# Layer 0's group roots as split pairs, parameters in the rows of the first input tile, the last norm's weight applied ahead of its root, and 500 tries in the planner

## The chip, the core and the metric

The kernel runs on one core of one Trainium2 chip. The metric is the device time of one execution in microseconds (us); lower is better. Each time given is the median of several executions. Beside it stands one profiled execution, whose rows are read below.

The engines have short names in the profile: PE is TensorE (matrix products into PSUM), PEld its weight loads, DVE is VectorE, ACT is ScalarE, POOL is GpSimd, SP is SyncE, which here issues nearly all DMAs.

## What is computed

A decoder trunk of two layers on 1024 tokens of 1024 channels in float32. Each layer: an RMS norm, one input projection whose columns feed four token mixers (a: latent attention, b: gated convolution, c: multi-scale pooling, d: sliding-window attention), an RMS norm of each mixer's 256 channels, one output projection, a residual; then an RMS norm, a gated feed-forward block, a residual. A last RMS norm ends it.

```python
for l in range(DEPTH):
    h = rmsnorm(x, attn_norm[l])
    proj = h @ w_in[l]
    ...
    groups = jnp.stack([y_a, y_b, y_c, y_d], axis=2)
    gf = groups.astype(jnp.float32)
    gf = gf * lax.rsqrt(jnp.mean(gf * gf, axis=-1, keepdims=True) + RMS_EPS)
    mixed = (gf.reshape(b, s, D_MIX) * mix_norm[l].astype(jnp.float32)).astype(x.dtype)
    x = x + mixed @ w_o[l]
    h2 = rmsnorm(x, ffn_norm[l])
    gate, up = jnp.split(h2 @ w_gate_up[l], 2, axis=-1)
    x = x + (jax.nn.silu(gate) * up) @ w_down[l]
return rmsnorm(x, final_norm)
```

## The kernel before

**Layout.** Channels lie on the 128 partitions, tokens on the free axis, in two halves of 512 (`HT`). A tile is 128x512 in float32, 256 KB. `x` is eight such tiles (`k`) in each half (`t`). Tiles live in 47 slots of 128x2x512 each (`u0` to `u46`); `F.pair()` takes a slot, `F.half()` half of one, and a half that is freed goes to the next caller.

**Split products.** A float32 value is carried as a pair: `hi`, the value cast to the fp32r type on ACT (L363, or L368 where a gain is multiplied in), and `lo`, the rest, made by a subtraction on DVE (L366, or L369 with the gain). `mm3` (L343) then makes each product of three: hi by hi, hi by lo, lo by hi. So nearly every PE row of the profile is L343.

**Norms.** `SumSq.add` squares tiles on ACT (L398, L407) and sums them on DVE (L415, and L409 for the last, which adds the epsilon). `rnorm` sums over the partitions by a product with a matrix of ones and then takes the reciprocal root: Ln, Exp and Square on ACT (L432 to L434), two steps on DVE (L435, L438). The document calls that product with ones the root's product. It has two forms. With `pair` false it is one product of plain float32 (L426). With `pair` true the sum is split into hi and lo first (ACT, then DVE), and two fp32r products with `ones_r` follow (L423). In layer 1 all group norms are pairs; in layer 0 group b is, while groups c and d (`group_scale`) and the query rank (`sq_q`) use the plain form, for each half of the tokens.

**Start.** A short series of products of ones (L562, 12 of them, two rows each in the trace) runs first on PE. SP loads half of two weight blocks (keys and values, `m` = 2, 3), the first x tile, a 128x86 table of parameters (`par`: gains, taps, sinks, final norm), then more x tiles, the other weight halves, the weights of `m` = 0 (queries) and the second half of x. ACT and DVE split each x tile with its gain from `par`; PE multiplies it by the key and value weights as it comes.

**End.** The last layer's last products run in two pieces of 256 tokens. After each piece: evacuation (L1792), the square (L429), the root's product (L426, L430), the root, and then `finish`: eight DVE steps that multiply a tile by its gain and the root (L490), with a DMA to the output for every two (L498).

**What sets the order.** The program is traced once, and a planner (`Order`) lays out the order of the instructions on each engine by a list schedule over modelled costs. `improve` then tries changed ranks: `tries` times it picks a modelled wait of PE, perturbs the ranks of the 45 us around it, and keeps the change if the modelled span is not longer. This runs twice (`SLOW`), and the better order is imposed on the program. DMA loads are instructions of SP, and their order is planned with the rest. SP has eight DMA lanes: the ninth issue waits until the first has landed.

Of the kernel before, what the change touches and what calls it, by code (L numbers as in the profile page):

```python
# [14 lines left out]
F32 = mybir.dt.float32  # L15
# [5 lines left out]
P = 128  # L21
# [23 lines left out]
WARM = 12  # L45
# [80 lines left out]
def trunk_kernel(ctx: ExitStack, tc: tile.TileContext, ins, out, given=None, ends=None):  # L126
# [17 lines left out]
    par = cpool.tile([P, L * PC_N + NK], F32, name="par")  # L144
# [236 lines left out]
    class SumSq:  # L381
# [35 lines left out]
        def rnorm(self, t, cols=whole, tag="t", final=None):  # L417
# [20 lines left out]
            dve.scalar_tensor_tensor(out=a, in0=q, scalar=1.5, in1=r0, op0=ALU.add, op1=ALU.mult)  # L438
            return self.acc[t]
# [16 lines left out]
    def enter_load(t, k):  # L456
        s = xf[k][t] = F.half()
        sp.dma_start(F.ap(s), x_in[k, :, t * HT : (t + 1) * HT])
# [10 lines left out]
    def first_half(w, i):  # L469

        s = F.half()
        sp.dma_start(F.ap(s), w[2][:, i * HT : (i + 1) * HT])
        w[3].append(s)

    def first_split(w, i):

        cs = slice(i * HT, (i + 1) * HT)
        split(R.ap2(w[0])[:, cs], R.ap2(w[1])[:, cs], F.ap(w[3][i]))
        F.free(w[3][i])

    def first_terms(w, t, k):
        hi, lo = (R.ap2(i)[:, k * P : (k + 1) * P] for i in w[:2])
        return [(hi, lo, R.ap(hh[k][t][0]), R.ap(hh[k][t][1]))]

    def finish(x, t, cols):

        for d in range(NK):
            a = F.ap(x[d][t])[:, cols]
            g = par[:, L * PC_N + d : L * PC_N + d + 1]
            dve.scalar_tensor_tensor(  # L490
                out=a, in0=a, scalar=g, in1=F.ap(ratt[t])[:, cols], op0=ALU.mult, op1=ALU.mult
            )
            ts = slice(t * HT + cols.start, t * HT + cols.stop)
            if t == 0:
                sp.dma_start(out[d, :, ts], a)
            elif d % 2:
                s = slots.cur[x[d][t] // 2]
                sp.dma_start(out[d - 1 : d + 1, :, ts].rearrange("d p n -> p d n"), s[:, :, cols])  # L498

    last_silu = None  # L500
    for l in range(L):
# [57 lines left out]
        if l == 0:  # L559
# [1791 lines left out]
```

## Time and profile before

| what | value |
|---|---|
| median of 3 runs (lowest to highest) | 2038.76 us (2038.35 to 2038.97) |
| the profiled execution, its own time | 2038.94 us |
| its span, from the first to the last instruction | 2037.2 us |
| PE busy / DVE / ACT / POOL | 99% / 76% / 50% / 28% of the span |
| PE instructions | 9422 products, 9422 weight loads |
| moved by DMA | 338.56 MB |
| granted TensorE clock | 0.999 |

How to read the views: the page gives busy times and the chain of work that ended last. The list of waits says which engine waited for which instruction. The timeline merges neighbouring instructions of one line; its columns are the start, the time from the first start to the last end, engine, line and operation, tiles written and read, shape, and the count. Ends of products are modelled, so that neighbouring products overlap in it: the step from one start to the next is what a product costs PE. Windows give the busy time of each engine in a stretch, with the count of instructions, the granted clock, the busy share of the DMA engines and the rate.

### The profile page before, as it was taken

Reading aid. Unit: us, or ns where it says so; the run is one execution under the profiler, and the core shown is the slowest. Engines: PE = TensorE matmul, PEld = TensorE weight load, DVE = VectorE, ACT = ScalarE, POOL = GpSimd, SP = SyncE. Lnnn points to the kernel's source line nnn. Section 1 sums busy time; section 2 is a strip of 40 time slices with the busy share of each in tenths; the row PEclk is TensorE's granted clock in tenths of the full one; section 3 lists DMA queues with packets and bytes.
Section 4 is the critical chain, followed back from the end, with each engine's and each line's share of the span. In section 5 each row is a group of like instructions: output and inputs, shape, how many; then the busy total and the mean of one; then the engine's idle time right before and its main releaser. Section 6 shows DMA issues by size and latency. Waiting matters only on the chain.

```text
span 2037.2 us, 26750 instructions
## 1 busy us (share of the span) xinstructions
PE 2023.3 (99%) x9422; PEld 1677.9 (82%) x9422; DVE 1543.7 (76%) x2449; ACT 1015.1 (50%) x1766; POOL 564.1 (28%) x428
## 2 busy tenths in 40 slices
PE   9999999999999999999999999999999999999998
PEld 7887888878888888888888878888888888888887
DVE  8779979997677778767646898889966766775555
ACT  7447657753333335555533676677433333354342
POOL 0100000047776783000001000000677777710000
PEclk9999999999999999999999999999999999999999
DMA  5531222434555556999835223242454555487552
GB/s 206 106 66 47 72 97 82 155 124 166 187 178 188 177 173 238 367 344 325 283 118 122 63 93 120 92 144 96 146 194 170 194 175 169 160 293 266 182 185 84
DMA packets 154231, 338.56 MB, mean 166 GB/s; under 512 B 15088, under 2 KB 62192, under 8 KB 154096
## 3 DMA queue, kind: packets, MB, share of 16 engines
q1 hardware_dynamic: 149616, 325.31, 46.3%
q0 software_dynamic: 4480, 11.54, 3.2%
q8 instruction: 74, 1.21, 0.2%
q14 instruction: 61, 0.50, 0.1%
HBM read 241.36 MB, written 105.91 MB: 170 GB/s over the span
## 4 chain that ended last, share of the span: by engine, by line
PE 97%; DVE 1%; issue 1%; ACT 0%; DMA 0%; POOL 0%; SPq 0%; DVEq 0%; ACTq 0%; POOLq 0%
PE ps_mm L343 38%; PE ps_s L343 29%; PE ps_t L343 12%; PE ps_pv L343 8%; PE ps_pv L1111 2%; PE ps_t L1099 1%; PE ps_s L1045 1%; PE ps_s L1047 1%; PE ps_s L1046 1%; PE ps_s L659 1%; PE ps_s L917 1%; PE ps_pv L720 1%; PE ps_t L708 1%; PE ps_t L423 0%; DVE u L366 0%
## 5 line engine op out<-in xcount | busy, mean ns | idle before, releaser
L343 PE MATMUL ps_mm<-u,u 128*128 128x512 f32 (+1 forms) x3378 | 831.9, 389 | 2.1 <-ACT u L368 0.7
L343 PEld LDWEIGHTS ps_mm<-u,u 128*128 128x128 f32 x3378 | 616.1, 188 | 125.4 <-issue 2.4
L343 PE MATMUL ps_s<-u,u 128*128 128x512 f32 x2670 | 636.4, 390 | 0.7 <-ACT u L1339 0.5
L366 DVE TENSOR_TENSOR u<-u,u 128x1024 fp32r<-128x1024 f32 (+3 forms) x429 | 493.8, 1174 | 187.4 <-ACT u L363 131.1
L363 ACT CAST u<-u 128x1024 fp32r<-128x1024 f32 (+3 forms) x429 | 370.6, 883 | 443.4 <-PE ps_mm L343 62.8
L343 PEld LDWEIGHTS ps_s<-u,u 128*128 128x128 f32 x2670 | 500.9, 188 | 107.0 <-ACT u L1339 1.3
L343 PE MATMUL ps_t<-u,u 128*128 128x512 f32 (+1 forms) x1124 | 256.3, 378 | 0.1
L343 PEld LDWEIGHTS ps_t<-u,u 128*128 128x128 f32 x1124 | 202.5, 188 | 40.8 <-DVE u L1515 1.5
L1523 POOL TENSOR_TENSOR tp<-tp,u 128x512 f32<-128x512 f32 x80 | 125.0, 1562 | 352.3 <-ACT tp L1521 215.9
L343 PE MATMUL ps_pv<-u,u 128*128 128x512 f32 x744 | 177.1, 389 | 0.0
L343 PEld LDWEIGHTS ps_pv<-u,u 128*128 128x128 f32 x744 | 139.7, 188 | 29.0
L317 POOL DMA_DIRECT2D gd<-in_w_gu x24 | 21.4, 894 | 415.8 <-PE ps_t L343 282.0
L1108 POOL MEMSET u<- 128x128 f32 x32 | 6.3, 223 | 427.4 <-PE ps_pv L1111 117.6
L1521 ACT ACTIVATE tp<-tp 128x512 f32<-128x512 f32 x80 | 50.6, 633 | 129.3 <-DVE tp L442 129.2
L363 ACT CAST u<-ps_t 128x512 fp32r<-128x512 f32 (+3 forms) x132 | 64.7, 503 | 55.4 <-PE ps_t L1099 29.1
L366 DVE TENSOR_TENSOR u<-ps_t,u 128x512 fp32r<-128x512 f32 (+3 forms) x132 | 74.7, 580 | 13.3 <-ACT u L363 12.4
L368 ACT ACTIVATE u<-u,par 128x512 fp32r<-128x512 f32 x100 | 70.2, 717 | 29.2 <-DVE u L442 9.1
L1601 POOL TENSOR_TENSOR u<-u 128x352 f32<-128x352 f32 x64 | 77.0, 1204 | 8.6 <-DMA u<-in_w_dn 8.1
L369 DVE SCALAR_TENSOR_TENSOR u<-u,par,u 128x512 fp32r<-128x512 f32 x100 | 73.2, 746 | 6.3 <-ACT u L368 6.2
L1311 POOL TENSOR_TENSOR u<-u 128x512 f32<-128x512 f32 x38 | 69.9, 1840 | 27.2 <-DVE u L366 25.3
L1601 POOL TENSOR_TENSOR u<-u,u 128x352 f32<-128x352 f32 x64 | 76.4, 1194 | 2.7
L442 DVE TENSOR_TENSOR tp<-tp,u 128x512 f32<-128x512 f32 x76 | 75.3, 990 | 2.0
(204 smaller groups left out, 2314.0 us busy)
## 6 DMA issues: line engine op xcount, KB each, us to landing
u<-in_w_gu SPq DMA_DIRECT2D x84, 512.0 KB, 4.0
ad<-u SPq DMA_DIRECT2D x154, 256.0 KB, 2.4
u<-ad SPq DMA_DIRECT2D x70, 512.0 KB, 5.8
u<-in_w_dn SPq DMA_DIRECT2D x64, 352.0 KB, 3.4
qd<-u SPq DMA_DIRECT2D x64, 352.0 KB, 3.5
u<-in_w_in SPq DMA_DIRECT2D x43, 512.0 KB, 5.3
u<-qd SPq DMA_DIRECT2D x32, 512.0 KB, 5.5
u<-in_w_dn SPq DMA_DIRECT2D x24, 512.0 KB, 5.4
```

Of the source, the lines that this page charges most:

```text
L317: paced(pool.dma_start(d, a, **more))
L343: last_mm = pe.matmul(o, w, r, start=start and k == 0 and i == 0, stop=stop and k == n - 1 and i == 2, skip_group_check=again,)
L363: a = act.copy(hi, f)
L366: dve.tensor_tensor(out=lo, in0=f, in1=rd(hi), op=ALU.subtract)
L368: a = act.activation(hi, f, AF.Copy, scale=gain)
L369: dve.scalar_tensor_tensor(out=lo, in0=f, scalar=gain, in1=rd(hi), op0=ALU.mult, op1=ALU.subtract)
L442: dve.tensor_tensor(out=o, in0=a, in1=b, op=ALU.mult)
L1111: pe.matmul(py[:, c0:], v_of(j, h), R.ap(s)[:, c0:], start=j == 0 and n == 0, stop=j == nj - 1 and n == 1,)
L1311: pool.tensor_tensor(out=q4, in0=q4, in1=F.ap(self.raw[1] + 1), op=ALU.add)
L1521: last_silu = act.activation(g, g, AF.Silu)
L1523: pool.tensor_tensor(out=g, in0=g, in1=r, op=ALU.mult)
L1601: pool.tensor_tensor(out=o, in0=a, in1=b, op=ALU.add)
```

## The change

Four things are changed. (1) Layer 0's groups c and d and the query rank use the pair form of the root's product. (2) `par` is no DMA of its own: its 86 columns stand in DRAM behind the 512 of the first x tile, one DMA loads both (`enter_first`), and DVE copies the columns to `par`. The key and value weights come as four blocks (`w_first[j]`) of two tiles' worth each, and the loads of the first half of x and of these blocks are held in one order by dependencies. Two products of ones fewer run ahead. (3) In the last norm's second half the gain is multiplied in on ACT ahead of the root (`gained`), and `finish_pairs` multiplies two tiles by the root in one DVE step. (4) The planner makes 500 tries, each resumed from a saved state, dropped early if PE is no further along, and kept only if the span is shorter.

```diff
-WARM = 12
+WARM = 10
...
+    def enter_first():
+        s = F.pair()
+        loads.append(sp.dma_start(F.ap2(s)[:, : HT + PC_ALL], ins["first"]))
+        xf[0][0] = s
+        got = F.ap(s + 1)[:, :PC_ALL]
+        hh[0][0] = half_split(F.ap(s), got[:, PC_ATTN : PC_ATTN + 1])
+        dve.tensor_copy(par, got)
+        F.free(s + 1)
...
-            wkv = [(R.pair(), R.pair(), ins["w_in"][0, m], []) for m in (2, 3)]
-            enter_load(0, 0)
-            sp.dma_start(par, ins["params"])
-            for i in range(2):
-                for w in wkv:
-                    first_half(w, i)
-                for k in range(4 * i, 4 * i + 4):
-                    if k:
-                        enter_load(0, k)
+            wkv, wraw, loads = [], [], []
+            for j in range(NK // 2):
+                wraw.append(F.half())
+                loads.append(sp.dma_start(F.ap(wraw[j]), ins["w_first"][j]))
+                if j == 0:
+                    wkv.append(half_split(F.ap(wraw[0])))
+                    F.free(wraw[0])
+                    enter_first()
+                else:
+                    loads.append(enter_load(0, 2 * j))
+                loads.append(enter_load(0, 2 * j + 1))
+            for a, b in zip(loads[1:], loads):
+                behind(a, b)
...
-            sg = SumSq(2 * P, g in ("b", "bcd")[l])
+            sg = SumSq(2 * P, g in "bcd")
...
-        sq_q = SumSq(2 * P, l > 0)
+        sq_q = SumSq(2 * P, True)
...
+    def gained(x, d, cols=whole):
+        a = F.ap(x[d][1])[:, cols]
+        act.activation(a, a, AF.Copy, scale=gain(d))
...
+    def finish_pairs(x, cols):
+        n = cols.stop - cols.start
+        r = F.ap(ratt[1])[:, cols].unsqueeze(1).to_broadcast([P, 2, n])
+        for m in range(NM):
+            s = slots.cur[x[2 * m][1] // 2][:, :, cols]
+            dve.tensor_tensor(out=s, in0=s, in1=r, op=ALU.mult)
+            ts = slice(HT + cols.start, HT + cols.stop)
+            sp.dma_start(out[2 * m : 2 * m + 2, :, ts].rearrange("d p n -> p d n"), s)
...
-            ratt[1] = ss.rnorm(1, cols, tag="s", final=F.ap(x[2 * NM - 2][1])[:, cols])
-            finish(x, 1, cols)
+            a = F.ap(x[2 * NM - 2][1])[:, cols]
+            ratt[1] = ss.rnorm(
+                1, cols, tag="s", final=a, behind=lambda: gained(x, 2 * NM - 2, cols)
+            )
+            finish_pairs(x, cols)
...
-            new = [
-                r + draw.gauss(0.0, 1) if at - 40 < t < at + 5 else r for r, t in zip(rank, end)
-            ]
-            e, o = self.run(new)
-            if max(e) <= span:
+            m = max(0, int((at - 40 * draw.random()) / self.STEP) - 1)
+            far = draw.choice((0.3, 1.0, 3.0))
+            a = marks[m][0]
+            new = [r + draw.gauss(0.0, far) if a < t < at + 5 else r for r, t in zip(rank, end)]
...
+            e, o = self.run(new, since=marks[m], marks=after)
+            if max(e) < span:
...
-            order = plan.improve(best, 30)[1]
+            order = plan.improve(best, 500)[1]
...
+    a["first"] = c(np.concatenate([a["xT"][0, :, :HT], lay.reshape(P, -1), fin], axis=1))
+    two = a["w_in"][0, 2:4].reshape(2, P, NK // 2, 2 * P)
+    a["w_first"] = c(two.transpose(2, 1, 0, 3)).reshape(NK // 2, P, HT)
```

The planner lays out the whole program anew, so nearly every row of every engine stands elsewhere. Three places follow; the names are the program's, with a number for each tile.

**SP, the first loads.** `in_w_in` are weights, `in_xT` tiles of x, `in_params` the table; in brackets stands what the issue waits for, a DMA lane or an engine. Before:

```order
L472 DMA u4_120<-in_w_in 128x512
L458 DMA u4_120<-in_xT 128x512
L565 DMA par_75<-in_params 128x86
L472 DMA u5_124<-in_w_in 128x512
L458 DMA u5_124<-in_xT 128x512
L458 DMA u6_127<-in_xT 128x512 x2
L472 DMA u7_130<-in_w_in 128x512
L458 DMA u8_133<-in_xT 128x512 [waits DMAHW0_49]
```

In the change, where `in_first` is x tile 0 with the table, `in_w_in` the 512 KB of query weights, and the tiles into `u8_138`, `u10_143`, `u11_146`, `u12_149` and `u13_152` are the second half of x:

```order
L580 DMA u0_114<-in_w_first 128x512
L467 DMA u2_119<-in_first 128x598
L591 DMA u9_140<-in_w_in 128x1024
L461 DMA u8_138<-in_xT 128x512
L461 DMA u10_143<-in_xT 128x512 x2
L461 DMA u11_146<-in_xT 128x512 x2
L461 DMA u12_149<-in_xT 128x512 [waits DMAHW0_49]
L461 DMA u12_149<-in_xT 128x512 [waits DMAHW1_49]
L461 DMA u13_152<-in_xT 128x512 [waits DMAHW2_49]
L461 DMA u2_119<-in_xT 128x512 [waits DMAHW3_49,DVE_49]
L580 DMA u4_126<-in_w_first 128x512 [waits DMAHW4_49]
```

The table's own DMA is gone. The second x tile of the first half goes to `u2_119`, the half slot that the table's columns leave: it waits for DVE to have read them, and stands behind the query weights and all eight tiles of the second half of x. The other loads of the first half are held behind it.

**PE, the root's product of group c, first half of the tokens.** `L659` and `L343` are products of the window attention and of a projection. Before:

```order
L659 MATMUL ps_s_1612<-u38_439,u8_1029 128x256
L659 MATMUL ps_s_1612<-u39_440,u8_1029 128x256
L426 MATMUL ps_t_1414<-u46_1409,ones_77 128x512
L659 MATMUL ps_s_1612<-u38_439,u8_1029 128x256
L659 MATMUL ps_s_1612<-u39_440,u8_1029 128x256
```

In the change:

```order
L344 MATMUL ps_mm_1571<-u29_331,u15_1307 128x512
L344 MATMUL ps_mm_1571<-u30_343,u21_1306 128x512
L424 MATMUL ps_t_1415<-u43_1412,ones_r_79 128x512 x2
L344 MATMUL ps_mm_1571<-u30_343,u21_1306 128x512
L344 MATMUL ps_mm_1571<-u30_343,u15_1307 128x512
```

One float32 product has become two fp32r products of the pair, among products of a projection.

**DVE, the end of the program.** Before:

```order
L435 SCALAR_TENSOR_TENSOR tn_18008<-ps_s_18002,tn_18008 128x256
L438 SCALAR_TENSOR_TENSOR u33_17221<-tn_18008,tn_18007 128x256
L490 SCALAR_TENSOR_TENSOR u3_16730<-u3_16730,par_75,u33_17221 128x256 x2
L490 SCALAR_TENSOR_TENSOR u18_16789<-u18_16789,par_75,u33_17221 128x256 x2
L490 SCALAR_TENSOR_TENSOR u44_16848<-u44_16848,par_75,u33_17221 128x256 x2
L490 SCALAR_TENSOR_TENSOR u27_16905<-u27_16905,par_75,u33_17221 128x256 x2
```

In the change:

```order
L436 SCALAR_TENSOR_TENSOR tn_18034<-ps_s_18028,tn_18034 128x256
L439 SCALAR_TENSOR_TENSOR u5_17240<-tn_18034,tn_18033 128x256
L510 TENSOR_TENSOR u25_16749<-u25_16749,u5_17240 128x2x256
L510 TENSOR_TENSOR u34_16808<-u34_16808,u5_17240 128x2x256
L510 TENSOR_TENSOR u42_16867<-u42_16867,u5_17240 128x2x256
L510 TENSOR_TENSOR u8_16924<-u8_16924,u5_17240 128x2x256
```

Four steps on two tiles stand where eight on one tile stood.

More of the change, by code (lines that the diff above doesn't have):

```diff
@@ L2054, in run @@
             t, e = best
+            if marks is not None and t >= self.STEP * len(marks):
+                state = t, left, ready, end, free, later, now, order, flying, served, port
+                marks.append(self.copied(state))
+            if until is not None and len(order["PE"]) == until:
+                return free["PE"]
             if fixed is not None:
@@ L2129, in improve @@
         draw = random.Random(1)
[L2130 to L2134 removed]
+        rank, _ = self.run([-x for x in best[2]], back=True)
+        marks = []
+        end, order = self.run(rank, marks=marks)
+        span = max(end)
         found = self.waits(order, end)
```

99 lines of the change are left out of this document (55 added, 44 removed).

## The prediction

> **What bounds the kernel now.** I read the page first: the span, the busy times and the chain that ended last.
>
> ```profile
> span 2037.2 us, 26750 instructions
> PE 2023.3 (99%) x9422; PEld 1677.9 (82%) x9422; DVE 1543.7 (76%) x2449; ACT 1015.1 (50%) x1766; POOL 564.1 (28%) x428
> PE 97%; DVE 1%; issue 1%; ACT 0%; DMA 0%; POOL 0%; SPq 0%; DVEq 0%; ACTq 0%; POOLq 0%
> ```
>
> PE is the bound nearly everywhere. Time can be won by giving PE less to do, by ending one of its waits, or at the two ends, where PE has nothing to do. The list of PE's waits over the whole execution says how much the second kind holds:
>
> ```profile
> PE ps_mm L343 <- ACT u L368: 0.7, 2, 0.6
> PE ps_mm L343 <- DVE tn L435: 0.6, 1, 0.6
> PE ps_s L430 <- ACT tn L429: 0.6, 1, 0.6
> PE ps_s L343 <- ACT u L1339: 0.5, 2, 0.3
> PE ps_mm L343 <- ACT u L363: 0.4, 1, 0.4
> PE ps_mm L343 <- DVE u L369: 0.3, 1, 0.3
> PE ps_s L343 <- DVE u L366: 0.2, 1, 0.2
> PE ps_s L1045 <- DVE te L442: 0.2, 1, 0.2
> ```
>
> Without the one at the end (L430, 0.6) these are 2.9 us. Ends of products are modelled, so that a delay shorter than the overlap doesn't show here; 2.9 is what can be seen of it. Windows by stage say where a new order could matter: layer 0's mixers, layer 1's, and a feed-forward stage.
>
> ```profile
> 43.00:432.00 389.00, 387.26 (x1895) 319.36 (x1894) 340.72 (x751) 243.25 (x525) 20.04 (x32) 1.00 0.31 90
> 1040.00:1440.00 400.00, 398.80 (x1963) 332.02 (x1963) 327.29 (x737) 245.49 (x529) 20.82 (x32) 1.00 0.36 107
> 1440.00:1805.00 365.00, 365.00 (x1610) 301.55 (x1609) 265.94 (x260) 130.67 (x178) 260.43 (x180) 1.00 0.52 178
> ```
>
> In the feed-forward stage PE is never idle (365.00 of 365.00); the mixers' stages have small gaps, and DVE is 88% busy in layer 0's (340.72 of 389).
>
> **The roots.** The price of a float32 root comes from the timeline, where one is followed by a long train of plain products. The last two rows are such a train with none in it.
>
> ```profile
> 184.69 1.02 PE L426 MATMUL ps_t<-u,ones 128*128 128x512 f32 x2
> 185.14 6.05 PE L343 MATMUL ps_mm<-u,u 128*128 128x512 f32 x24
> 191.05 1.12 PE L426 MATMUL ps_t<-u,ones 128*128 128x512 f32 x2
> ...
> 36.99 5.62 PE L343 MATMUL ps_t<-u,u 128*128 128x512 f32 x24
> 42.44 0.60 PE L635 MATMUL ps_t<-cst,te 128*128 128x128 f32 x4
> ```
>
> From 36.99 to 42.44 there are 24 products: 0.227 us each. From 184.69 to 191.05 there are 6.36 us for a root and 24 products (5.45): the root costs 0.91. Two fp32r products cost 0.45, so each replaced root gives PE 0.45 back. Six are replaced (groups c and d and the query rank, two halves of the tokens): **-2.7 us**. What hides the added splits: a cast on ACT and a subtraction on DVE for each root, priced by the rows of such tiles at the start,
>
> ```profile
> 7.08 0.60 ACT L363 CAST u<-u 128x512 fp32r<-128x512 f32 x1
> 7.72 0.69 DVE L366 TENSOR_TENSOR u<-u,u 128x512 fp32r<-128x512 f32 x1 [0.28 <-ACT u L363]
> ```
>
> 1.29 us ahead of each root's product, 0.84 net on the root's own chain. What waits for these roots are the splits of the mixed groups, used only when the output projection begins, and the queries' scale; PE has projections and window attention to do meanwhile. If that cover is gone, 1.29 us a root comes back (a rival below). DVE gets 4.1 us more in a stage where it has 48 to spare.
>
> **The start.** Here the chain of waits begins with the table of parameters:
>
> ```profile
> 1.67 4.18 DMA par<-in_params
> ...
> 5.94 0.73 ACT u L368
> 6.69 0.76 DVE u L369
> ```
>
> The table is 43 KB and lands at 5.85; x tile 0 had landed before it, and its gain is in the table, so the first real product starts at 6.71. The change brings both in one DMA. I walk through the new order with these rows:
>
> ```profile
> 1.06 5.49 PE L562 MATMUL ps_pv<-ones 128*128 128x128 f32 x24 [1.06 <-DVE ones L148]
> 3.49 0.62 ACT L363 CAST u<-u 128x512 fp32r<-128x512 f32 x1 [1.47 <-DMA u<-in_w_in]
> ...
> 19.51 1.93 ACT L368 ACTIVATE u<-u,par 128x512 fp32r<-128x512 f32 x3
> 19.96 4.06 DVE L369 SCALAR_TENSOR_TENSOR u<-u,par,u 128x512 fp32r<-128x512 f32 x6
> ```
>
> ```profile
> L458 SPq DMA_DIRECT2D u<-in_xT x16: 328/328/432, 1.2 to 14.4; - x16
> ...
> DMA to landing us min/median/max: 2.9/5.9/6.0
> ```
>
> ```profile
> 4.00:7.00 3.00, 2.84 (x13) 2.54 (x12) 1.38 (x6) 1.17 (x3) 0.00 (x0) 1.00 0.90 248
> 12.00:14.00 2.00, 2.00 (x10) 1.68 (x9) 2.00 (x4) 2.00 (x4) 0.00 (x0) 1.00 1.02 407
> ```
>
> The x tile issued at 1.20 landed 2.9 later at the earliest, at 4.1. At 407 GB/s, a tile (262 KB) takes 0.64 us; the first load is now 306 KB, 0.11 more: 4.2. Behind it come the query weights (524 KB, to 5.5), eight tiles of the second half of x (to 10.7), and only then tile 1 of the first half (11.3): its issue waits for DVE's last read of the table's columns (about 5.9) and for a lane (the first of the eight, 6.2), and what is in flight is served first. All other loads of the first half are queued behind it on SP.
>
> PE can begin when 20 passes of ones are done (20/24 of 5.49: at 5.6), 1.1 earlier than now. What it can do before tile 1 is there: 6 products of tile 0, 12 of the second half's tiles 0 and 1, 3 query products. These 21 (4.8 us) wait in turn for DVE (tile 0's lo to 5.9, the 1024-wide query lo to 7.9, two tiles' lo 0.66 apart) and end near 10.9. Tile 1's hi needs 0.72 on ACT, free of the eight tiles before it (0.6 apart) at 11.6: PE goes on at 12.4, **a new wait of 1.4 to 1.5**. From there DVE sets the pace: seven subtractions (0.66), seven sums and three weight subtractions (0.6 each) are 10.6 us, which puts the first norm's root product near 23.4.
>
> Before, that root started at 20.41, with this ahead of it:
>
> ```profile
> 6.70:20.41 13.71, 13.65 (x55) 10.11 (x55) 1.00 1.04 389
> ```
>
> 55 products, 12.5 us, so 7.9 us of the time had gone to nothing. In the new order 69 products (15.7) stand ahead of it: 23.4 less 15.7 is 7.7 to 7.8. The earlier start is given back by the wait for tile 1: **-0.1 us**. Bounds: if the queue served only 248 GB/s to 7 us, as it now does with the table in it, tile 1 would land 1.2 later (+1.2); if the second half's tiles cost nothing because PE found all its work among them, the full 1.1 would stay (-1.2). I take the middle, since the walk's steps are all rows of this stretch.
>
> A rule speaks against the combined load: the Trainium skill, "DMA: Bandwidth & Descriptors", section "How a descriptor splits into AXI transactions", has a row that doesn't begin at a multiple of 256 B fetch from the boundary below. Rows of 2392 B mostly don't; by it I estimate up to a tenth more, 0.07 us on the first load, against nothing by bytes. No row before shows such a load.
>
> **The end.** After the last root come eight DVE steps of 256 columns, and the output DMAs:
>
> ```profile
> 2028.18 0.38 ACT L432 ACTIVATE tn<-ps_s 128x256 f32<-128x256 f32 x1 [0.79 <-PE ps_s L430]
> 2030.48 3.26 DVE L490 SCALAR_TENSOR_TENSOR u<-u,par,u 128x256 f32<-128x256 f32 x8
> 2031.39 2.75 SPq L498 DMA_DIRECT2D out<-u  x4
> ```
>
> Now four steps of 2x256 run. No such step is in the trace; the nearest is a product of two tiles in SBUF of 512 columns:
>
> ```profile
> 158.04 1.28 DVE L442 TENSOR_TENSOR u<-u,u 128x512 f32<-128x512 f32 x2
> L442 DVE TENSOR_TENSOR u<-u,u x46: 668/683/1459, 134.5 to 1450.8; 128x512 f32<-128x512 f32 x46
> ```
>
> 0.60 apart and 0.68 long: 2.48 in place of 3.26, -0.8. The DMAs (0.64 each) now come as fast as they drain, which costs the last some 0.15 us: **-0.6 us**, with bounds of -0.8 and, if the repeated operand is as slow as two steps of L490, 0. The gain of the last tile, 0.42 on ACT, is put between the square and Ln, where ACT is idle for 0.79: nothing; without that gap it would be +0.4.
>
> **The new order.** 500 tries in place of 30 look for shorter waits of PE in a model of the program. The trace shows 2.9 us of such waits outside the start and the end. I take half, **-1.5 us**. Bounds: all of it and as much of the delays that don't show (-5), or as much again in new waits, since an order that leaves less slack by the model has less for what the model misses (+2).
>
> **The sum**, from the profiled execution's own 2038.94 (its span is 2037.2): 2038.94 - 2.7 - 0.1 - 0.6 - 1.5 = 2034.0. The median of the runs is 0.2 lower, so I predict **2033.9 us**.
>
> **Rivals.** *The order gives much more.* The named waits end, and short delays with them: 2038.8 - 3.4 - 6 = 2029.4. For it: gaps are spread over two mixers' stages. Against: what the list names is 2.9.
>
> *The start loses.* Tile 1 lands at 12.5, and the plan gives nothing: 2038.8 - 2.7 - 0.6 + 1.3 + 0.5 of new waits = 2037.3. For it: 248 GB/s in 4 to 7 us. Against: the small table is gone from the queue. By the Trainium skill, "TensorE: Matmul & The Clock Gate", section "What's actually happening", PE idle for about 3.4 us falls to half its clock until it has been busy as long; by that a wait 2 us longer than mine would cost another 1.7 as an estimate. The rows here have a clock of 1.00 throughout, and no such wait.
>
> *The splits are exposed: slower than before.* At each of the six roots PE stands until the pair is there. The point is where less than 1.29 us of other products lies in PE's order between the end of the sum and the root; then each costs 1.29, 7.7 in all: 2038.8 - 2.7 - 0.6 + 7.7 = 2043.2. For it: DVE is 88% busy, and a queued DVE makes the pair later still. Against: the planner sees these steps, and the new order places other products beside them.
>
> *It doesn't do what it says.* The roots shrink, but PE waits at these places anyway for the sum: only the end remains, 2038.2.
>
> **How the numbers follow.** Forecast (2031.5 to 2036) 0.50; much more 0.17; the start loses 0.17; exposed splits 0.10; nothing from the roots 0.06. Within 0.2% is about what a measurement of this kernel can tell from no change; it is 4.1 us, from 2034.7 to 2042.8. Seven tenths of the forecast's case lie below that, so faster is 0.35 + 0.17 = 0.52. Slower is the exposed splits and 0.01 of the start, 0.11; the rest, 0.37, is the same. The range 2028.5 to 2039 leaves out the exposed splits, the best part of the second case and the worst of the third.
>
> **What would show it.** In the changed kernel's profile: no 43 KB load, the first real product near 5.6, a wait of PE for ACT near 11 to 12.4, the first norm's root near 23.4; six pairs of root rows among plain products without idle before them; four DVE steps 0.6 apart at the end, and 0.6 less from Ln's start to the last instruction; a list of waits shorter than 2.9 us in the mixers. It is wrong if PE's idle time there grows by over 4 us, or if tile 1's wait is over 3 us.

## The result, and the profile after

| what | before | after |
|---|---|---|
| median (15 runs each) | 2038.76 us | 2042.88 us |
| lowest to highest | 2037.87 to 2039.17 | 2040.48 to 2044.40 |
| after / before, 95% interval | | 1.0020 (1.0014 to 1.0026) |
| the profiled execution, its own time | 2038.94 us | 2044.40 us |
| its span | 2037.2 us | 2042.6 us |

The change makes the kernel 4.1 us slower; 4.9 us faster was forecast. The profiled execution is the slowest of the 15, so its rows show 1.5 us more than the median. Runs of after also spread over 3.9 us, those of before over 1.3; the last section has what is known of that.

The page of after, to be held against the three lines of before:

```profile
span 2042.6 us, 26766 instructions
PE 2023.7 (99%) x9418; PEld 1677.0 (82%) x9418; DVE 1546.8 (76%) x2448; ACT 1023.6 (50%) x1784; POOL 569.5 (28%) x428
PE 95%; DVE 3%; ACT 1%; issue 1%; DMA 0%; SPq 0%; DVEq 0%; ACTq 0%
```

PE's share of the last chain falls from 97% to 95%, DVE's rises from 1% to 3%. Lines from 344 on have moved: L364/L367 are now the cast and the subtraction of a split, L369/L370 those with a gain, L424 the pair root, L427 the float32 one. The list of PE's waits was to get shorter:

```profile
PE ps_mm L344 <- ACT u L369: 1.9, 1, 1.9
PE ps_t L344 <- DVE u L1534: 1.4, 4, 0.5
PE ps_s L344 <- ACT u L369: 1.2, 1, 1.2
PE ps_s L344 <- DVE tp L1758: 1.1, 2, 0.9
PE ps_mm L344 <- DVE tn L436: 0.8, 1, 0.8
```

The first is the start. L1534 and L1758 are steps of the feed-forward block (the negated product that empties a bank of PSUM, and the gate's sum), where PE waited for nothing before.

A list of waits misses delays that overlap a modelled end. So I counted PE's work in each trace, product by product (a product of 512 columns 0.227 us, others by their columns, the ones at the start nothing), and asked at equal work done how much later than before PE starts its next product. The answers are good to some 0.2 us. Columns: work done; the times in before at which these points lie are 6.7, 49, 174, 260, 469, 1030, 1486 and 2022 us. In work done, layer 0's mixers end at about 400, its feed-forward stage at 975, layer 1's mixers at 1395, its feed-forward stage at 1955.

```
work (us)    0    40   160   240   440  1000  1440  1975 | median
after     -1.0  +3.1  +2.4  +2.2  +0.5  +1.4  +1.3  +5.6 | 2042.88
e1        -0.0  -0.2  +1.9  +1.8  +3.2  +3.2  +7.5  +8.2 | 2047.56
e2        -1.0  +3.5  +2.7  +2.5  +1.0  +0.9  +1.1  +2.0 | 2040.55
e3        -0.7  -0.2  -0.8  +2.1  +2.2  +2.6  +3.2  +3.5 | 2041.73
e4        -1.4  -0.5  -1.5  +1.5  +0.1  +1.3  +1.8  +2.0 | 2038.41
e5        -0.5  -0.2  -0.3  -0.2  -0.2  +1.4  +1.6  +3.6 | 2042.83
e6        -0.9  +2.1  +3.1  +4.6  +6.3  +7.7 +11.6 +11.6 | 2050.59
e7        -0.6  -0.1  -0.6  +2.3  +2.2  +3.3  +3.9  +4.5 | 2043.28
e8        -1.4  -1.2  -1.7  -0.2  -1.9  -1.6  -0.8  -0.3 | 2039.08
e9        -1.6  -1.3  -1.3  -2.2  -1.8  -2.0  -1.6  -0.7 | 2037.76
e10       -1.4  -2.1  -2.5  -2.0  -3.4  -3.7  -3.7  -3.7 | 2035.86
e11       -0.0  -0.2  -0.5  -0.5  -0.5  -0.5  +3.5  +4.7 | 2044.83
e12       -1.7  -1.3  -1.8  +1.1  +1.5  +1.2  +7.8  +8.9 | 2047.69
e13       -1.0  +2.2  +1.4  +0.9  -0.8  -1.0  -0.8  -0.7 | 2038.28
e14       -1.7  -0.3  +0.2  -1.0  -0.9  -0.9  -0.3  -0.1 | 2038.54
e15       -1.2  -1.4  -2.0  -1.2  -2.9  -3.3  -2.7  -2.6 | 2037.01
e16       -1.4  -1.3  -1.8  -1.2  -3.1  -2.9  -2.6  -2.3 | 2036.74
```

The row of after: PE begins 1.0 early, is 3.1 late once the keys' and values' products are done, makes up 2.6 in layer 0's mixers, loses 0.9 in its feed-forward block and 4.3 in layer 1's.

**The start.** The timeline of after, first SP's first x tiles and what ACT makes of them, then PE; and the one issue of x tile 1, alone, with its time to landing:

```profile
2.14 6.10 SPq L461 DMA_DIRECT2D u<-in_xT  x9
4.79 0.21 DVE L471 COPY par<-u 128x86 f32<-128x86 f32 x1
7.92 6.26 ACT L369 ACTIVATE u<-u,par 128x512 fp32r<-128x512 f32 x9
...
11.53 0.84 PE L344 MATMUL ps_s<-u,u 128*128 128x512 f32 x3
14.22 0.50 PE L344 MATMUL ps_mm<-u,u 128*128 128x512 f32 x1 [1.85 <-ACT u L369]
```

```profile
L461 SPq DMA_DIRECT2D u<-in_xT x1: 328/328/328, 7.9 to 7.9; - x1
DMA to landing us min/median/max: 5.5/5.5/5.5
```

Tile 1 is the ninth of nine x tiles on SP's queue. It is issued at 7.9, since eight lanes are in flight, and lands at 13.4, 0.68 after the tile ahead of it; ACT takes the tiles as they land, and PE stands until 14.22. What the stand does to the clock shows in windows that begin and end where the recorded clock changes (length; busy time and count of PE, PEld, DVE, ACT, POOL; granted clock; share of the DMA engines; GB/s):

```profile
12.14:15.55 3.41, 1.56 (x7) 0.97 (x6) 2.94 (x6) 3.41 (x7) 0.00 (x0) 1.00 1.05 388
15.55:18.96 3.41, 3.41 (x9) 2.64 (x8) 3.41 (x7) 3.41 (x7) 0.00 (x0) 0.50 1.06 394
18.96:22.37 3.41, 3.41 (x16) 2.79 (x15) 3.41 (x7) 3.41 (x7) 0.00 (x0) 1.00 1.02 412
```

PE was busy for 1.56 of 3.41 us; for the next 3.41 the clock is 0.50, and nine products fit in place of 16. The first norm's root starts at 26.98, before at 20.41.

**The roots.** A replaced root, on the timeline, among plain products without idle:

```profile
152.59 0.70 PE L344 MATMUL ps_mm<-u,u 128*128 128x512 f32 x2
153.13 0.62 PE L424 MATMUL ps_t<-u,ones_r 128*128 128x512 f32 x2
153.59 2.22 PE L344 MATMUL ps_mm<-u,u 128*128 128x512 f32 x9
```

From 153.13 to 153.59 is 0.46 for a root, as forecast. What is left of this at the place shows in more points of the same count. All six replaced roots lie between 125 and 200 of work; a float32 root counts as much as a pair, so that a cheaper root shows as a gain. After, e8 and e10 have pairs there, e9 and e14 float32 roots:

```
work (us)   40   125   200   300   440
after     +3.1  +3.3  +2.6  +2.3  +0.5
e8        -1.2  -1.0  +0.3  -0.2  -1.9
e9        -1.3  -1.1  -1.7  -2.4  -1.8
e10       -2.1  -1.7  -1.7  -1.9  -3.4
e14       -0.3   0.0  -0.2  -1.2  -0.9
```

In the change PE gains 0.7 there, not 2.7. Between 140 and 220 us its list of waits has 1.5 (the 1.2 for ACT in the list above, at 182 us, and 0.3 for DVE); before has none there. So much of what the pairs save goes into waits. The larger part of the 2.6, 1.8 us, comes after 300, where no edit changed a root. Before has waits of 0.8 in its list there and after none; what else makes up these 1.8 isn't shown.

**The end.** The timeline from Ln on, and one window of the drain:

```profile
2033.67 0.38 ACT L433 ACTIVATE tn<-ps_s 128x256 f32<-128x256 f32 x1 [0.25 <-PE ps_s L431]
2035.97 2.50 DVE L510 TENSOR_TENSOR u<-u,u 128x512 f32<-128x512 f32 x4
2037.05 1.97 SPq L512 DMA_DIRECT2D out<-u  x4
```

```profile
2039.00:2040.00 1.00, 0.00 (x0) 0.00 (x0) 0.00 (x0) 0.00 (x0) 0.00 (x0) 0.50 1.01 348
```

The DVE steps take 2.50 (forecast 2.48). But the first output DMA is issued 3.38 after Ln's start (3.21 before) and lands at 5.70 (5.70 before); the DMA engines are then full, and the outputs land 0.72 to 0.78 apart, the last at 7.92 (8.02 before). From Ln to the end of the span: 8.99 before (2037.17 - 2028.18), 8.96 after. This isn't the same in all orders: over all traces the stretch takes 8.97 to 9.03 with the old end and 8.46 to 9.05 with the new one. In e10 (8.54) the first DMA is issued 0.07 after its DVE step ends, in after 0.39; what holds it there isn't shown.

**The feed-forward block.** One group in layer 1, the same in both traces. Before:

```profile
1598.52 2.88 PE L343 MATMUL ps_mm<-u,u 128*128 128x512 f32 x12
1601.44 0.69 DVE L1739 TENSOR_TENSOR tp<-ps_mm,tn 128x512 f32<-128x512 f32 x1 [1.92 <-PE ps_mm L343]
1603.09 1.74 POOL L1283 TENSOR_TENSOR u<-u,u 128x512 f32<-128x512 f32 x1
1603.96 2.89 PE L343 MATMUL ps_s<-u,u 128*128 128x512 f32 x12
1603.99 1.92 DVE L366 TENSOR_TENSOR u<-u,u 128x1024 fp32r<-128x1024 f32 x1 [0.32 <-PE ps_pv L343]
1605.84 0.68 DVE L1515 SCALAR_TENSOR_TENSOR u<-ps_pv,tp 128x512 f32<-128x512 f32 x1
1606.68 0.63 PE L343 MATMUL ps_t<-u,u 128*128 128x512 f32 x2
```

After:

```profile
1599.85 2.43 PE L344 MATMUL ps_mm<-u,u 128*128 128x512 f32 x10
1602.11 0.39 PE L344 MATMUL ps_pv<-u,u 128*128 128x512 f32 x1
1602.34 0.61 PE L344 MATMUL ps_mm<-u,u 128*128 128x512 f32 x2
1605.29 2.65 PE L344 MATMUL ps_s<-u,u 128*128 128x512 f32 x11
1605.30 1.29 POOL L1302 TENSOR_TENSOR u<-u,u 128x512 f32<-128x512 f32 x1
1605.32 2.36 DVE L367 TENSOR_TENSOR u<-u,u 128x1024 fp32r<-128x1024 f32 x1 [0.78 <-PE ps_pv L344]
1607.60 0.68 DVE L1534 SCALAR_TENSOR_TENSOR u<-ps_pv,tp 128x512 f32<-128x512 f32 x1
1608.33 0.50 PE L344 MATMUL ps_t<-u,u 128*128 128x512 f32 x1 [0.39 <-DVE u L1534]
```

DVE's wide subtraction and then L1515 begin when the products of `ps_pv` end; the products of `ps_s` cover them. Before, L1515 ends at 1606.52 and PE, behind 12 of these products, goes on at 1606.68: 0.16 us of slack. After, only 11 of them stand ahead of `ps_t`: 0.23 less cover. And the wide subtraction takes 2.36, because it starts 0.02 after a POOL step of two operands: that one ends at 1606.59, and the subtraction needs 1.1 from there. Before, it took 1.92 by the same count: the POOL step beside it had begun 0.9 earlier and ended at 1604.83, and the subtraction again needed 1.1 from there. L1534 ends at 1608.28, and PE loses 0.55 from start to start. The lists name 2.5 us of such waits in the two feed-forward blocks, this group's among them; the table has 5.2 there, and the rest hides under modelled ends. By the Trainium skill, "SBUF — State Buffer", section "SBUF: two separate sides", a DVE step with two operands in SBUF and a GpSimd step lock each other out, and whichever starts first keeps the ports for the whole instruction; these rows agree, to 0.1 us.

### The profile page after: what moved, and what is told of

It is laid out like the page before. It is cut to its first block, busy times and chain, and to the rows that moved or that the text cites. A ratio compares the mean times of both kernels' runs of the same rounds, so it can differ in the third digit from the quotient of the medians.

```text
span 2042.6 us, 26766 instructions
## 1 busy us (share of the span) xinstructions
PE 2023.7 (99%) x9418; PEld 1677.0 (82%) x9418; DVE 1546.8 (76%) x2448; ACT 1023.6 (50%) x1784; POOL 569.5 (28%) x428
## 4 chain that ended last, share of the span: by engine, by line
PE 95%; DVE 3%; ACT 1%; issue 1%; DMA 0%; SPq 0%; DVEq 0%; ACTq 0%
PE ps_mm L344 37%; PE ps_s L344 29%; PE ps_t L344 12%; PE ps_pv L344 8%; PE ps_pv L1130 2%; PE ps_t L1118 1%; DVE u L367 1%; PE ps_s L1064 1%; PE ps_s L1066 1%; PE ps_s L1065 1%; PE ps_s L678 1%; PE ps_s L936 1%; PE ps_pv L739 1%; PE ps_t L727 1%; PE ps_t L424 1%
## 5 line engine op out<-in xcount | busy, mean ns | idle before, releaser
L344 PE MATMUL ps_s<-u,u 128*128 128x512 f32 x2670 | 643.0, 390 | 1.8 <-DVE tp L1758 1.1
L367 DVE TENSOR_TENSOR u<-u,u 128x1024 fp32r<-128x1024 f32 (+3 forms) x435 | 493.6, 1156 | 184.2 <-ACT u L364 119.5
L364 ACT CAST u<-u 128x1024 fp32r<-128x1024 f32 (+3 forms) x435 | 374.4, 879 | 456.5 <-PE ps_s L344 68.2
L364 ACT CAST u<-ps_t 128x512 fp32r<-128x512 f32 (+3 forms) x132 | 64.8, 505 | 50.0 <-PE ps_t L1118 27.9
L367 DVE TENSOR_TENSOR u<-ps_t,u 128x512 fp32r<-128x512 f32 (+3 forms) x132 | 75.1, 580 | 16.1 <-ACT u L364 14.9
L369 ACT ACTIVATE u<-u,par 128x512 fp32r<-128x512 f32 x99 | 69.8, 719 | 29.2 <-DVE u L445 14.0
L1620 POOL TENSOR_TENSOR u<-u,u 128x352 f32<-128x352 f32 x64 | 80.5, 1257 | 3.3 <-DMA u<-in_w_dn 0.9
L370 DVE SCALAR_TENSOR_TENSOR u<-u,par,u 128x512 fp32r<-128x512 f32 x99 | 72.3, 745 | 5.6 <-ACT u L369 5.5
```

Source lines behind the costliest of these rows:

```text
L344: last_mm = pe.matmul(o, w, r, start=start and k == 0 and i == 0, stop=stop and k == n - 1 and i == 2, skip_group_check=again,)
L364: a = act.copy(hi, f)
L367: dve.tensor_tensor(out=lo, in0=f, in1=rd(hi), op=ALU.subtract)
L369: a = act.activation(hi, f, AF.Copy, scale=gain)
L370: dve.scalar_tensor_tensor(out=lo, in0=f, scalar=gain, in1=rd(hi), op0=ALU.mult, op1=ALU.subtract)
L1620: pool.tensor_tensor(out=o, in0=a, in1=b, op=ALU.add)
```

## The experiments

Lower-case e and a number name the runs; all are timed beside the kernel before, 2038.8 to 2038.9 in each set. Every edit lets the planner lay out the program anew, so the total says less than the table's row at the place of the edit.

**The search alone** (the new search in the kernel before; the line of its edit that sets the tries):

```diff
-            order = plan.improve(best, 30)[1]
+            order = plan.improve(best, 500)[1]
```

> Only the planner's new search (500 tries, each kept only where the planned end comes earlier); no edit of the start, the roots or the end. Theory A (the new order itself spoils the feed-forward stages: products wait there for DVE steps whose slack the planner used up): PE loses 3 to 6 us in layer 1's feed-forward stage, gains 0 to 2 in layer 0's mixers, 2040.5 to 2043.5. Theory B (the feed-forward loss follows from the shifted start and the other edits, not from the search): no new waits after 1440 us, 2036.5 to 2038.5.

Measured 2047.56, ratio 1.0044 (1.0031 to 1.0056). Slower by more than either theory had, and in the mixers (+3.4 between 40 and 440, +4.3 between 1000 and 1440), which neither expected. The planner makes one plan with DVE and ACT at their modelled speed and one with both 3% slower, and takes the better by its own trials: in before the second, here the first. So this run changed two things at once.

```diff
-SLOW = (1.0, 1.03)
+SLOW = (1.03,)
```

> The kernel before with the new search, planned only with DVE and ACT taken 3% slower than measured (the planner makes one plan without that margin and one with it, and takes the better by its own trials; before, the one with the margin was taken, in the run of the search alone the one without). Theory C (the 8.8 us of that run came from the flip to the plan without margin; the search itself is harmless): 2037 to 2039.5. Theory A (the search uses up the slack of DVE steps whichever plan it works on): 2041 to 2044, with new waits of PE for DVE in a feed-forward stage.

Measured 2042.83, ratio 1.0020 (1.0011 to 1.0029). Layer 0's mixers are as before (-0.2 at 440); 1.6 is lost in its feed-forward block and 2.0 in layer 1's. So with the margin the search by itself costs 4.0 us here, all of it in the feed-forward blocks: theory A. The waits that show there, in its lists between 440 and 1000 us and between 1445 and 2000 us:

```profile
PE ps_s L343 <- DVE tp L1739: 0.2, 1, 0.2
PE ps_t L343 <- DVE u L1515: 1.0, 1, 1.0
```

```diff
-SLOW = (1.0, 1.03)
+SLOW = (1.0,)
```

> The kernel before with its old search (30 tries), planned only without the 3% margin on DVE and ACT. Theory C: the missing margin alone costs most of the 8.8: 2043 to 2048. Theory A: without the new search nothing is lost: 2038 to 2040.

Measured 2050.59, ratio 1.0056 (1.0042 to 1.0069): theory C holds too. Both runs without the margin lose in the mixers; what e1 lost goes with that plan (8.8 with 500 tries, 11.8 with 30). In that plan the new search gains 3.0; with the margin it costs 4.0.

**All edits, the old search** (`improve` with 30 tries, as in before).

> All edits of the change (start, roots, end) with the planner as it was (30 tries). Theory A: the feed-forward stages stay clean as before, the start still loses 3.3 (x tile 1 lands at 13.4, the granted clock falls to 0.5), the roots give 2.7, the end 0.1: 2038.8 + 3.3 - 2.7 - 0.1 = 2039.3, within 1. Theory B: the feed-forward loss of 5 stays: 2043 to 2045.

Measured 2040.55, ratio 1.0008 (0.9999 to 1.0017); 2039.3 within 1 was expected, so the sum misses by 1.3. The start loses 3.5, the mixers give 2.5, and of after's 4.3 in the last feed-forward block 0.9 is left. Against this run, the new search costs the change 2.3 (2042.88 - 2040.55).

**The search kept out of the feed-forward blocks,** nothing else changed in the change itself:

```diff
-        return found
+        return [f for f in found if f[0] < 430 or 1000 < f[0] < 1440]
...
-SLOW = (1.0, 1.03)
+SLOW = (1.03,)
```

> The change as it is, with the search's tries aimed only at the mixers (and the 3% margin, as the change's plan had). Theory A (the tries aimed at the feed-forward stages make the change's loss there): of the 0.9 lost between 440 and 1000 us and the 4.2 after 1440, against before, less than 1 in all is left; the start's 3.1 to 4 stays: 2042.9 - 4.5 = 2038.4, within 1. Rival (the feed-forward loss follows from the other edits): 2041.5 to 2043.5.

Measured 2038.28 (2036.81 to 2038.84), ratio 0.9996 (0.9987 to 1.0005). Between 440 and 1000 PE loses -0.2, after 1440 +0.1. The windows of layer 1's last blocks, in after and then in this run, show PE's busy time:

```profile
1440.00:1998.00 558.00, 555.79 (x2442) 457.18 (x2442) 384.40 (x396) 217.09 (x289) 264.18 (x182) 1.00 0.56 192
```

```profile
1440.00:1998.00 558.00, 557.95 (x2480) 462.29 (x2479) 381.19 (x401) 220.41 (x294) 260.11 (x180) 1.00 0.57 192
```

For the same edits, the search without tries aimed at the feed-forward blocks is 4.6 us better (2042.88 - 2038.28). Of the 6.1 between the two profiled executions 5.3 lie in these blocks.

**The start undone** (separate table, weights and `WARM` of before; roots, end and 500 tries stay).

```diff
-                    enter_first()
+            enter_load(0, 0)
+            sp.dma_start(par, ins["params"])
```

> The change with its start undone (roots, end and the new search stay). If the start is what costs 3.3 to 4.3 us: 2042.9 - 3.4 = 2039.5 with the feed-forward loss, and 2035 to 2036 where this plan has none; granted clock 1.00 in the first 30 us and the first norm's root at 20 to 21 us. Rival (the start is neutral, the loss is the search's): 2042 to 2043.5.

Measured 2041.73, ratio 1.0015 (1.0006 to 1.0023). The start is as before (-0.2 at 40), so its 3.3 are back, but 2.9 go between 160 and 240, in layer 0's latent attention. By the total the rival is nearer; by the row at the place, the start costs what was said.

**Tile 1 in a slot of its own.** `F.free` of the table's half and of the first weights comes after the loads of the first half have their slots:

```diff
-                    F.free(wraw[0])
                     enter_first()
...
-        F.free(s + 1)
...
+            F.free(wraw[0])
+            F.free(xf[0][0] + 1)
             for a, b in zip(loads[1:], loads):
```

> The change with one edit at the start: the two slots that the first weights and the table's columns came in are given back only after the loads of the first half have their slots, so x tile 1 needn't wait for DVE and stands third on SP's queue instead of twelfth. If the late tile 1 is the cause of the start's loss: tile 1 lands near 6, no wait of PE over 1 us and a clock of 1.00 in the first 30 us, the first norm's root at 19.5 to 21.5 in place of 27, and 2042.9 - 4 = 2038 to 2040 if the feed-forward loss stays. Rival (the start is late because the combined load and DVE's pace are late): the root at 25 or later, less than 1 us gained.

Measured 2038.41 (2036.61 to 2040.93), ratio 0.9999 (0.9990 to 1.0008). The first norm's root:

```profile
19.97 1.02 PE L427 MATMUL ps_t<-u,ones 128*128 128x512 f32 x2
```

19.97 in place of 26.98, and 3.6 less lateness at 40. With the old search:

> All edits of the change with x tile 1 in a slot of its own, and the search of before. Roots -2.7, end -0.1, the start as in the run with the new search (0.5 ahead of before at the same amount of work): 2038.8 - 3.3 = 2035.5, within 0.8. Rival (as there, a hole of 3 to 4 us in layer 0's mixers before the mixed groups' products, because the pairs of the roots are late): 2038 to 2040.

Measured 2039.08, ratio 1.0001 (0.9993 to 1.0010): the rival's hole is there, 3.0 us in the list of waits. PE on the timeline, with the cast that its last wait ends on:

```profile
175.74 0.71 PE L424 MATMUL ps_t<-u,ones_r 128*128 128x512 f32 x2 [1.07 <-DVE u L756]
176.97 0.73 PE L953 MATMUL ps_t<-u,e_r 128*128 128x512 f32 x2 [0.52 <-DVE tn L436]
178.02 1.03 ACT L238 CAST u<-u 128x1024 fp32r<-128x1024 f32 x1
179.11 1.20 PE L344 MATMUL ps_mm<-u,u 128*128 128x512 f32 x4 [1.41 <-ACT u L238]
```

PE's next projection waits for its weights, whose cast (L238) ACT has behind the casts and root steps of the norms.

**The roots left in float32,** in that kernel:

```diff
-            sg = SumSq(2 * P, g in "bcd")
+            sg = SumSq(2 * P, g in ("b", "bcd")[l])
...
-        sq_q = SumSq(2 * P, True)
+        sq_q = SumSq(2 * P, l > 0)
```

> As the run with all edits, x tile 1 in its own slot and the old search (2039.1), but with the six roots left in float32; planned with the 3% margin, as that one was. There PE stands 3.5 us at 175 to 179 us in front of the pair roots and of what follows them. Theory D (the added splits on the roots' chain are what PE stands for: exposed splits): no gap over 0.5 us at 165 to 190 us; six roots dearer by 0.45, the hole cheaper by 3.5: 2038 to 2039. Rival E (the hole is a matter of the order and of DVE's queue, not of the splits): a gap of 2 us or more stays there, 2041 to 2042.5.

Measured 2037.76, ratio 0.9995 (0.9987 to 1.0004). The same place has no gap:

```profile
174.97 0.62 PE L424 MATMUL ps_t<-u,ones_r 128*128 128x512 f32 x2
175.43 2.25 PE L344 MATMUL ps_mm<-u,u 128*128 128x512 f32 x9
177.52 0.62 PE L953 MATMUL ps_t<-u,e_r 128*128 128x512 f32 x2
177.98 2.48 PE L344 MATMUL ps_mm<-u,u 128*128 128x512 f32 x10
```

Theory D: the hole is there with the pairs and not without them, and with this search the pairs cost more than they give (1.3). None of e8's three waits ends on a pair's own cast or subtraction; they end on other steps of ACT and DVE. That the added splits push these back is argued from the comparison, not seen in a row. With the search aimed at the mixers, both come again:

> All edits, x tile 1 in its own slot, margin of 3%, 500 tries, but the search aims only at PE's planned waits in the two layers' mixers, none in the feed-forward stages. Theory A (the tries aimed at the feed-forward stages spend real slack there): the 1.4 us that the same kernel with the unrestricted search lost between 480 and 1000 us (against before) and 0.2 after 1440 go to within 0.3 of nought; 2036 to 2037.5. Rival (the feed-forward stages lose the same without being aimed at): 2038 to 2039.5.

> As the fastest version so far (x tile 1 in its own slot, tries aimed at the mixers, 2035.9), with the six roots in float32. If the pair roots still give their 2.7: 2038 to 2039. If the stand in front of them eats half or more of it: 2036.5 to 2037.5. If they cost as much as they give: 2035 to 2036.5.

With pairs (e10) 2035.86, ratio 0.9985 (0.9976 to 0.9994); with float32 roots (e14) 2038.54, ratio 0.9998 (0.9989 to 1.0006). The runs are 2.7 apart, just what was forecast for the roots, but not at the roots. At 40 of work, ahead of the first of them, the two profiled executions are 1.8 apart already; between 125 and 200, where all six lie, the one with pairs gains nothing and the other 0.2. And e10 beats both kernels, by 2.9 and 7.0 us: all edits, tile 1 in its own slot, the search out of the feed-forward blocks.

**Another seed,** `random.Random(2)`:

> As the fastest version so far, with another seed of the search. If aiming at the mixers is what helped: 2035 to 2037.5. If it was the draw: 2037.5 to 2041, with new waits in the mixers.

Measured 2036.74, ratio 0.9990 (0.9981 to 0.9999): one more draw, 0.9 behind the first and still ahead of before.

**Roots and end alone, search and start of before.**

> The change's roots and end with the start and the search of before. Roots -2.7 and end -0.1: 2038.8 - 2.8 = 2036.0, within 0.8. Rival (a new order of any kind loses some us elsewhere, so that the gain of the roots doesn't show): 2037.5 to 2040, with the loss in places that no edit touches.

Measured 2043.28, ratio 1.0024 (1.0014 to 1.0033), 7.3 over the forecast. As in e3, 2.9 go between 160 and 240, and 1.7 in the two feed-forward blocks, in places that no edit touches. What makes that order of the latent attention bad isn't settled.

**More margin,** `SLOW = (1.06,)`, in before and in the kernel of e8:

> The kernel before, old search, planned with DVE and ACT taken 6% slower instead of 3%. Without margin it took 2050.6, with 3% 2038.8. If slack for DVE and ACT is what an order is good or bad by: 2036.5 to 2038.5. Rival (3% is about what the chip needs, more only spreads PE's work worse): 2039 to 2043.

> All edits, x tile 1 in its own slot, old search, planned with a margin of 6% instead of 3%. If slack is what matters, the hole at 175 to 179 us shrinks below 1 us: 2035.5 to 2037.5. Rival (the hole is made by something that the margin doesn't touch): 2038.5 to 2041.

Measured 2044.83, ratio 1.0031 (1.0020 to 1.0041), and 2047.69, ratio 1.0041 (1.0029 to 1.0054). Slack is not all that an order is good by: with 6% layer 1's mixers lose 4.0 and 6.6. The waits at the hole of e8 halve (1.4 in the list, 3.0 there), but don't fall below 1 us.

**Rows of 2560 B** for the combined load, in the kernel of e10:

```diff
-        loads.append(sp.dma_start(F.ap2(s)[:, : HT + PC_ALL], ins["first"]))
+        loads.append(sp.dma_start(F.ap2(s)[:, : HT + PC_ROW], ins["first"]))
```

with `PC_ROW = 128` and zeros behind the table's columns.

> As the fastest version so far, with the rows of the combined first load filled up from 598 to 640 values (2392 to 2560 B, a multiple of 256 B). There the first load landed 1.0 us after the weights ahead of it, 0.78 by bytes at the rate of the x tiles. If rows off a 256 B boundary cost the difference: 0.85 or less, for 7% more bytes. If not: 1.0 to 1.1. The whole: 2035 to 2037 either way.

Measured 2037.01, ratio 0.9991 (0.9982 to 1.0000). The load lands 0.79 after the weights with either length; by bytes, at the rate of the later tiles, it would be 0.78 for the short rows and 0.84 for the long ones. The same short rows took 1.0 in e4 and 1.4 in after, so these two are not the rows. The rule that the prediction cites (the Trainium skill, "DMA: Bandwidth & Descriptors", "How a descriptor splits into AXI transactions") would add some 0.07 to the short rows by its estimate; a difference of that size can't be told here.

**What the search does from kernel to kernel.** Five pairs of runs differ in the search alone. 500 tries in place of 30 cost 4.0 us in the kernel before (e5) and 2.3 in the change (against e2); they gain 0.7 with tile 1 in its own slot (e4, e8), 1.5 with the start of before (e3, e7) and 3.0 without the margin (e1, e6). In all of these but e1 and e6 the planner took the plan with the margin. In the two feed-forward blocks, by the table, the five runs with 500 free tries lose 5.2, 3.6, 1.4, 0.7 and 0.7 (after, e5, e4, e3, e1), the seven with 30 tries 0.7 to 1.7, the five with aimed tries 0.5 at most. So free tries can spoil these blocks, and aimed ones didn't. How much they spoil changes with the program, and no other seed of a free search was run.

## Why the prediction was wrong

**The new order, -1.5, was the step that failed most.** It read the search as a way to shorten waits, bounded its harm by +2, and looked for it in the mixers. Measured: +2.3 in the change (against e2), +4.0 in the kernel before (e5). By the rows, the change loses 5.2 in the feed-forward blocks, where the same edits lose 0.8 with the old search (e2) and nothing with aimed tries (e13). The window that was quoted, PE busy 365.00 of 365.00, was read as a stage with nothing to win; it also said that anything the planner moved there could only lose. The rows show how little slack was left (0.16 us).

**The start, -0.1, failed by its walk.** Its chain was right: the new wait for tile 1 came, by the releaser that was named. Its sizes were not. The combined load landed 0.6 later than walked, the query weights 1.3, tile 1 2.1 (13.4 against 11.3). The walk took 407 GB/s from the first load on. From 3.33 to 8.70 us 1.35 MB landed, that is 252 GB/s, about the 248 of the row quoted for 4 to 7 us; from there on a tile took 0.67. The bound for this, +1.2, let the slow rate end at 7 us. That tile 1 is issued at 7.9 in place of 6.2 adds nothing, since it lands right behind the tile ahead of it. The walk's last step also has a slip: 12.4 and 10.6 are 23.0, not 23.4. So the rival "the start loses" had the mechanism, and its price was too small: it put tile 1 at 12.5 and the loss at 1.3. The lateness at 40 is 2.2 in e13, where tile 1 landed at 14.2 and the clock stayed at 1.00, and 3.1 in after. The slot alone (e10 against e13) is worth 2.4.

**The clock was waved aside.** The prediction said that no row had such a wait. Its own forecast had one of 1.5 us, with thin work around it. That was enough in after and e2; in e13 PE waited for 1.6 and the clock held.

**The roots, -2.7: the price was right, the cover was not.** Each replaced root costs PE 0.46 in place of 0.91. But of the 2.7 the change keeps 0.7 where the roots are, with 1.5 of new waits there; the prediction had the added splits hidden under projections and window attention. That after makes up 2.6 between 40 and 440, and that e10 and e14 are 2.7 apart, is luck: most of both lies elsewhere. So the rival of exposed splits is real, at 2.0 of its 7.7; with the search of e8 the pairs cost 1.3 more than they give.

**The end, -0.6, was 0.03 here,** and at most 0.5 in other orders. The DVE part was right to 0.02 us. What failed is the first output's landing, which came no earlier than before, and the 0.15 for DMAs that come as fast as they drain: the term used the rate of loads (0.64 for 256 KB) for stores that landed 0.72 to 0.78 apart.

In sum, by the rows of after: +3.3 (start, at 125) - 0.7 (where the roots are) - 2.1 (the rest of layer 0's mixers) + 5.2 (feed-forward blocks) - 0.1 (layer 1's mixers) + 0 (end) = 5.6, against 5.5 between the two profiled executions (2044.40 - 2038.94). Differences of whole runs give no such sum: with the old search the new start gains 2.7 (e2 against e7), with the new one it costs 1.2 (after against e3), because each run is planned anew.

## What to carry to other kernels

Where an engine is already busy all the time in a stage, an order from a model has little to win there and can lose: aim a search at stages in which the trace, not the model, shows waits, and keep the margin under which the last good order was made. Undoing one edit of a kernel whose order is planned re-plans all of it; compare traces at equal work done, place by place, before believing the totals. When two things share a buffer, ask what the queue will place ahead of the one that now has to wait, and at what rate that will land. When a total agrees with a forecast, look whether its time lies where the edit is: here two totals agreed with the roots' 2.7, and most of their time lay elsewhere.

## What the runs showed of the hardware

**The clock is set in stretches of 3.41 us, and a thin stretch is enough.** All recorded changes of the granted clock lie whole multiples of 3.41 us apart (10.24, 3.41 and 6.83 us in after and e4). For every such stretch of the 18 traces in which the clock was 1.00, I counted for how much of it PE passed columns: 0.227 us for 512 columns, twice that in plain float32, where a root of two rows takes 0.91. After each stretch with less than 0.37 the clock was 0.50: 0.31 in e2, 0.35 in after and e4, 0.36 in e12, and the others at the end of the program, where PE runs out of work. After each one with 0.38 or more it stayed at 1.00: 0.38 in e5, 0.40 in e15, 0.41 in e8, 0.42 in e3, 0.45 in e13. So in these traces the limit lies between 0.37 and 0.38 by this count. The longest single wait in after's stretch was 1.85 us. By the Trainium skill, "TensorE: Matmul & The Clock Gate", section "What's actually happening", the gate looks at free-running windows of about 3.4 us, and an idle one halves the clock; the length agrees, but the four stretches named first were not idle.

**Whether a hole costs clock differs from run to run.** In e4 and in e8 PE has nearly the same hole; windows along the recorded stretches, e4 and then e8:

```profile
174.47:177.88 3.41, 1.88 (x6) 0.61 (x5) 3.35 (x6) 2.63 (x6) 0.00 (x0) 1.00 0.13 54
177.88:184.71 6.83, 6.17 (x15) 4.84 (x16) 5.86 (x9) 4.09 (x8) 0.00 (x0) 0.50 0.18 41
```

```profile
173.47:176.88 3.41, 1.91 (x8) 0.96 (x6) 3.29 (x6) 2.73 (x6) 0.00 (x0) 1.00 0.31 119
176.88:180.29 3.41, 1.91 (x7) 1.01 (x7) 3.21 (x6) 3.39 (x7) 0.00 (x0) 1.00 0.02 5
```

In e4 one stretch is thin and two slow ones follow; in e8 two share the hole, and the clock holds. The runs of e4 fit: at a mean clock of 0.999 they took 2036.61 to 2037.41 us, at 0.998 2037.67 to 2039.83, at 0.996 2040.93. For after it isn't enough: its fastest run, 2040.48, had 0.997, and one of 2043.61 had 0.999. What spreads those runs stays open.

**A clock of 1.00 before the first record means nothing.** Products of ones at the start step by 213 ns, and in e3 by 111 ns from 4.98 us on, where its clock record begins: its first 5 us run at half the clock though the windows print 1.00.
